# Batched matrix product on one core: x rounded to float16 before its transposes, two values to a float32 word

## The chip, the core and the metric

One core of a Trainium2 chip runs the whole program. Its TensorE (PE) multiplies and transposes, VectorE (DVE) and ScalarE (ACT) convert and copy, SyncE (SP) issues all transfers between the chip's memory (DRAM) and the core's own SBUF, and PSUM holds what TensorE writes. The metric is the device time of one execution in microseconds (us). Five executions of the kernel before took 135.75 to 136.54 us, median 136.04 us.

## What is computed

```python
def setup_inputs():
    batch, dim_i, dim_j, dim_k = 32, 256, 512, 384
    return {
        "x": np.random.randn(batch, dim_i, dim_j).astype(np.float32),
        "y": np.random.randn(batch, dim_j, dim_k).astype(np.float32),
    }

def reference(x, y):
    return np.einsum('bij,bjk->bik', x, y).astype(np.float32)
```

For each of 32 batches, a 256 x 512 matrix x times a 512 x 384 matrix y gives a 256 x 384 matrix. In float32 that is 16.8 MB of x, 25.2 MB of y and 12.6 MB of output, 54.5 MB in all.

## The kernel before

TensorE contracts over partitions, so both factors need j on the partitions. y comes from DRAM that way: partition p of a loaded y holds rows j = 4p to 4p+3, called t = 0 to 3 (NJ = 4). x arrives with rows i on the partitions and has to be transposed. Both are rounded to float16 on the way, the products add up in float32.

**Tiles.** x is loaded for four batches at a time (a quad q, 0 to 7): `x_sb`, 128 partitions by 8 rows (R = 8) by 512 columns, 2 MB in one transfer, line 66, three buffers. y is loaded for two batches (a step's pair u, 0 to 15), one transfer of 768 KB for each batch, line 81, five buffers `y_sb`. The output of a pair is one transfer of 768 KB, line 150, from `o_sb`.

**Transposes.** `transpose(q, half)`, lines 87 to 108, makes 16 transposes of 128 x 128 float32 for half of the four t (line 99): the columns j = 4c + t of one row r of `x_sb`, a stride of four elements. Four of them fill one PSUM tile `t_ps` (four buffers, 512 float32 per partition, one bank), and one copy takes the tile to `xt_sb` and rounds it to float16: DVE takes the even tiles (line 105), ACT the odd ones (line 107). A half has four tiles, so two copies on each engine.

**The rest of a step.** `round_y(u)` casts y to float16 in eight pieces of 384 columns, four on ACT (line 116) and four on DVE (line 118). `multiply(u)` makes 32 matmuls (line 130) into four PSUM tiles `o_ps` (four buffers): the two batches of the pair use the left and the right half of the array side by side, with 64 columns of `xt_sb` as weights each. `collect(u)` copies the four `o_ps` to `o_sb`, e = 0 and 2 on ACT (line 143), e = 1 and 3 on DVE (line 145). `store(u)` issues the output.

**Order.** Every instruction goes through `keep`, so each engine runs its own in the order of the source. Step s (0 to 17) does: load y of pair s+2 (with x of quad (s+3)/2 ahead of it when s is odd), collect(s-2), multiply(s-1), round_y(s), the first half of the next quad's transposes when s is odd and the second half when s is even and over 0, store(s-2). At s = 0 both halves of quad 0 come ahead of everything else. SP issues loads and stores in that one order: a store that waits for its copies holds back the loads behind it. There are eight semaphores for transfers, used in turn, so each issue also waits until the transfer eight places before it has landed.

**The end.** The last load issued is y of pair 15. Behind it stand five stores, of pairs 11 to 15. The last transposes are half 1 of quad 7, in step 14; after them come multiply(14), multiply(15), and their collects and stores.

Of the kernel before, what the change touches and what calls it, by code (L numbers as in the profile page):

```python
# [1 line left out]

# [5 lines left out]


MM_DT = mybir.dt.float16  # L10
F32 = mybir.dt.float32
P = 128


Q = 4
G = 2

LAG = 4


@with_exitstack
def kernel(
    ctx: ExitStack,
    tc: tile.TileContext,
    x: bass.AP,
    y: bass.AP,
    out: bass.AP,
):
    nc = tc.nc

    B, I, J = x.shape
    _, _, K = y.shape


    M = P // G
    NE = I // M
    NJ = J // P

    PQ = P // Q
    R = I // PQ
    H = R // NE
    U = B // G

    const_pool = ctx.enter_context(tc.tile_pool(name="const", bufs=1))
    x_pool = ctx.enter_context(tc.tile_pool(name="x_pool", bufs=3))
    y_pool = ctx.enter_context(tc.tile_pool(name="y_pool", bufs=5))
    yr_pool = ctx.enter_context(tc.tile_pool(name="yr_pool", bufs=2))
    xt_pool = ctx.enter_context(tc.tile_pool(name="xt_pool", bufs=2))  # L50
    o_pool = ctx.enter_context(tc.tile_pool(name="o_pool", bufs=5))
    tpsum_pool = ctx.enter_context(tc.tile_pool(name="tpsum", bufs=4, space=bass.MemoryType.PSUM))
    opsum_pool = ctx.enter_context(tc.tile_pool(name="opsum", bufs=4, space=bass.MemoryType.PSUM))


    keep = tc.keep_in_program_order

    identity = const_pool.tile([P, P], F32)
    make_identity(nc, identity)

    x_of, y_of, yr_of, xt_of, ps_of, o_of = {}, {}, {}, {}, {}, {}

    def load_x(q):
        x_of[q] = x_pool.tile([P, R, J], F32, name="x_sb")
        keep(
            nc.sync.dma_start(
                out=x_of[q],
                in_=x[q * Q : (q + 1) * Q].rearrange("g (p r) j -> (g p) r j", r=R),
            )
        )  # L70

    def load(u):

        if u == 0:
            load_x(0)
        if (u + 1) * G % Q == 0 and u + 1 < U:
            load_x((u + 1) * G // Q)
        y_of[u] = y_pool.tile([P, G, NJ, K], F32, name="y_sb")
        for g in range(G):
            keep(  # L80
                nc.sync.dma_start(
                    out=y_of[u][:, g],
                    in_=y[u * G + g].rearrange("(q t) k -> q t k", q=P),
                )
            )

    def transpose(q, half):

        x_sb = x_of[q]
        if half == 0:  # L90
            xt_of[q] = xt_pool.tile([P, NJ, NE, Q * PQ, H], MM_DT, name="xt_sb")
        n = 0
        for t in range(half * NJ // 2, (half + 1) * NJ // 2):
            for e in range(0, NE, 2):
                t_ps = tpsum_pool.tile([P, 2, H, Q * PQ], F32, name="t_ps")
                for f in range(2):
                    for h in range(H):
                        keep(
                            nc.tensor.transpose(  # L99
                                t_ps[:, f, h], x_sb[:, h * NE + e + f, t::NJ], identity  # L100
                            )
                        )
                dst = xt_of[q][:, t, e : e + 2].rearrange("c f p h -> c f h p")
                if n % 2 == 0:
                    keep(nc.vector.tensor_copy(dst, t_ps))  # L105
                else:
                    keep(nc.scalar.copy(dst, t_ps))  # L107
                n += 1

    def round_y(u):  # L110
        y_sb = y_of.pop(u)
        yr_of[u] = yr_pool.tile([P, G, NJ, K], MM_DT, name="y_r")
        for g in range(G):
            for t in range(NJ):
                if t % 2 == 0:
                    keep(nc.scalar.copy(yr_of[u][:, g, t], y_sb[:, g, t]))  # L116
                else:
                    keep(nc.vector.tensor_copy(yr_of[u][:, g, t], y_sb[:, g, t]))  # L118

    def multiply(u):  # L120
        xt_sb, y_r = xt_of[u * G // Q], yr_of.pop(u)
        ps_of[u] = []
        for e in range(NE):
            o_ps = opsum_pool.tile([P, K], F32, name="o_ps")
            ps_of[u].append(o_ps)
            for t in range(NJ):
                for g in range(G):
                    a = (u * G + g) % Q
                    keep(
                        nc.tensor.matmul(  # L130
                            o_ps[g * M : (g + 1) * M],
                            xt_sb[:, t, e, a * PQ : (a + 1) * PQ].rearrange("c p h -> c (p h)"),
                            y_r[:, g, t],
                            start=(t == 0),
                            stop=(t == NJ - 1),
                        )
                    )

    def collect(u):
        o_of[u] = o_pool.tile([P, NE, K], F32, name="o_sb")  # L140
        for e in range(NE):
            if e % 2 == 0:
                keep(nc.scalar.copy(o_of[u][:, e], ps_of[u][e]))  # L143
            else:
                keep(nc.vector.tensor_copy(o_of[u][:, e], ps_of[u][e]))  # L145
        del ps_of[u]

    def store(u):
        keep(
            nc.sync.dma_start(  # L150
                out=out[u * G : (u + 1) * G].rearrange("g (m e) k -> (g m) e k", e=NE),
                in_=o_of.pop(u),
            )
        )


    ahead = LAG - 2
    for u in range(ahead):
        load(u)
    for s in range(U + 2):  # L160
        if s + ahead < U:
            load(s + ahead)
        if s == 0:
            transpose(0, 0)
            transpose(0, 1)
        if s >= 2:
            collect(s - 2)
        if 1 <= s <= U:
            multiply(s - 1)
        if s < U:  # L170
            round_y(s)
        for half in range(2):
            q = (s + 1 - half) * G // Q
            if (s + 1 - half) * G % Q == 0 and 0 < q < B // Q:
                transpose(q, half)
        if s >= 2:
            store(s - 2)


# [1 line left out]
_INS = ['x', 'y']  # L181
_OUTS = [((32, 256, 384), 'float32')]


# [23 lines left out]
```

## Time and profile before

| what | value |
|---|---|
| median of 5 runs | 136.04 us |
| the profiled execution's own time | 135.99 us |
| its span in the trace | 134.1 us |
| granted TensorE clock, mean | 0.906 |
| bytes moved, mean rate over the span | 54.65 MB, 407 GB/s |
| L130 matmuls, 512 | 54.9 us busy |
| L99 transposes, 256 | 37.0 us busy |
| L118 / L116 casts of y, 128x384, 64 each | 20.0 us DVE, 355 ns each / 29.5 us ACT, 513 ns each |
| L105 / L107 copies of t_ps, 128x512, 32 each | 22.5 us DVE, 728 ns each / 22.4 us ACT, 731 ns each |
| L145 / L143 copies of o_ps, 128x384, 32 each | 16.3 us DVE, 543 ns each / 13.9 us ACT, 492 ns each |

The span runs from the first to the last event that the profiler recorded on the core; the execution's own time is 1.89 us longer. Busy time of an engine is the sum of its instructions' times, so two engines can both be busy at once. Times in the trace below are counted from the start of the span. A DMA share of 1 means that all 16 DMA engines that serve the core are moving data; rounding and overlap take it to 1.02 or so when none rests.

### The profile page before, as it was taken

Reading aid. Unit: us, or ns where it says so; the run is one execution under the profiler, and the core shown is the slowest. Engines: PE = TensorE matmul, PEld = TensorE weight load, DVE = VectorE, ACT = ScalarE, POOL = GpSimd, SP = SyncE. Lnnn points to the kernel's source line nnn. Section 1 sums busy time; section 2 is a strip of 40 time slices with the busy share of each in tenths; the row PEclk is TensorE's granted clock in tenths of the full one; section 3 lists DMA queues with packets and bytes.
Section 4 is the critical chain, followed back from the end, with each engine's and each line's share of the span. In section 5 each row is a group of like instructions: output and inputs, shape, how many; then the busy total and the mean of one; then the engine's idle time right before and its main releaser. Section 6 shows DMA issues by size and latency. Waiting matters only on the chain.

```text
span 134.1 us, 1968 instructions
## 1 busy us (share of the span) xinstructions
PE 91.0 (68%) x768; PEld 74.7 (56%) x768; DVE 56.2 (42%) x128; ACT 63.9 (48%) x129; POOL 0.7 (1%) x6
## 2 busy tenths in 40 slices
PE   0049494979199767786099771997739976597920
PEld 0049474868177666666077661676626766476810
DVE  0004617471743365701735318324273334628520
ACT  3004837662762476712744428424375245737710
POOL 2000000000000000000000000000000000000000
PEclk9999999999959999999968996589975799779997
DMA  5999999999999999999999999999999999999994
GB/s 112 410 407 453 401 423 421 440 405 416 410 459 393 419 425 420 449 399 418 423 437 439 400 421 429 441 425 404 427 418 456 399 417 425 418 432 416 425 396 169
DMA packets 8073, 54.65 MB, mean 407 GB/s; under 512 B 896, under 2 KB 896, under 8 KB 7040
## 3 DMA queue, kind: packets, MB, share of 16 engines
q1 hardware_dynamic: 8064, 54.53, 97.9%
q8 instruction: 6, 0.10, 0.3%
q14 instruction: 3, 0.02, 0.0%
HBM read 41.94 MB, written 12.58 MB: 407 GB/s over the span
## 4 chain that ended last, share of the span: by engine, by line
DMA 78%; PE 13%; ACT 4%; DVE 0%; issue 0%
DMA y_sb<-in_y_dram 40%; DMA x_sb<-in_x_dram 38%; PE o_ps L130 9%; PE t_ps L99 3%; ACT xt_sb L107 2%; ACT y_r L116 1%; ACT o_sb L143 1%; DVE o_sb L145 0%
## 5 line engine op out<-in xcount | busy, mean ns | idle before, releaser
L130 PE MATMUL o_ps<-y_r,xt_sb 128*64 128x384 f16 x512 | 54.9, 376 | 27.5 <-ACT o_sb L143 19.7
L130 PEld LDWEIGHTS <-xt_sb 128*64 128x64 f16 x512 | 40.4, 125 | 38.6 <-issue 21.4
L116 ACT CAST y_r<-y_sb 128x384 f16<-128x384 f32 x64 | 29.5, 513 | 36.5 <-DMA y_sb<-in_y_dram 36.3
L99 PE MATMUL t_ps<-identity,x_sb 128*128 128x128 f32 x256 | 37.0, 302 | 9.9 <-DMA x_sb<-in_x_dram 9.9
L99 PEld LDWEIGHTS t_ps<-identity,x_sb 128*128 128x128 f32 x256 | 34.3, 212 | 14.7 <-issue 14.7
L118 DVE CAST y_r<-y_sb 128x384 f16<-128x384 f32 x64 | 20.0, 355 | 44.4 <-DMA y_sb<-in_y_dram 44.4
L107 ACT CAST xt_sb<-t_ps 128x512 f16<-128x512 f32 x32 | 22.4, 731 | 25.9 <-PE t_ps L99 25.9
L105 DVE CAST xt_sb<-t_ps 128x512 f16<-128x512 f32 x32 | 22.5, 728 | 26.2 <-PE t_ps L99 26.2
L145 DVE COPY o_sb<-o_ps 128x384 f32<-128x384 f32 x32 | 16.3, 543 | 2.1 <-PE o_ps L130 2.1
L143 ACT COPY o_sb<-o_ps 128x384 f32<-128x384 f32 x32 | 13.9, 492 | 1.3 <-PE o_ps L130 1.3
L107 ACT ACT_TABLE_LOAD x1 | 1.3, 1283 | 0.7 <-PEq L192 0.7
masks.py:199 POOL TENSOR_SCALAR_AFFINE_SELECT identity<-identity 128x128 f32<-128x128 f32 x1 | 0.3, 294 | 0.1
masks.py:197 POOL MEMSET identity<- 128x128 f32 x1 | 0.2, 205 | 0.3 <-POOLq L192 0.3
L192 POOL MEMSET const-bfloat16-1.0<- 128x1 bf16 x1 | 0.1, 102 | 0.0
L192 POOL MEMSET const-uint8-127<- 128x1 uint8 x1 | 0.1, 102 | 0.0
L192 POOL MEMSET const-float32-0.0<- 128x1 f32 x1 | 0.1, 99 | 0.2 <-issue 0.2
L192 POOL MEMSET const-float32-1.0<- 128x1 f32 x1 | 0.1, 99 | 0.0
## 6 DMA issues: line engine op xcount, KB each, us to landing
y_sb<-in_y_dram SPq DMA_DIRECT2D x32, 768.0 KB, 17.9
x_sb<-in_x_dram SPq DMA_DIRECT2D x8, 2048.0 KB, 20.9
out_dram<-o_sb SPq DMA_DIRECT2D x16, 768.0 KB, 17.9
```

The costliest lines, as they stand in the source:

```text
L99: nc.tensor.transpose(t_ps[:, f, h], x_sb[:, h * NE + e + f, t::NJ], identity)
L105: keep(nc.vector.tensor_copy(dst, t_ps))
L107: keep(nc.scalar.copy(dst, t_ps))
L116: keep(nc.scalar.copy(yr_of[u][:, g, t], y_sb[:, g, t]))
L118: keep(nc.vector.tensor_copy(yr_of[u][:, g, t], y_sb[:, g, t]))
L130: nc.tensor.matmul(o_ps[g * M : (g + 1) * M], xt_sb[:, t, e, a * PQ : (a + 1) * PQ].rearrange("c p h -> c (p h)"), y_r[:, g, t], start=(t ...
L143: keep(nc.scalar.copy(o_of[u][:, e], ps_of[u][e]))
L145: keep(nc.vector.tensor_copy(o_of[u][:, e], ps_of[u][e]))
L192: nc = _bacc.Bacc("TRN2", target_bir_lowering=False, num_devices=1)
```

## The change

x of a quad is cast to float16 as soon as it is there, into a new tile `x_r` (two buffers): four casts of two rows, 128 x 1024 each, two on DVE and two on ACT. For quads 1 to 7 they stand in the odd steps ahead of round_y; for quad 0 they stand first. `x_r` is then read as float32 words, each of two neighbouring float16 values (j = 4c + 2n and 4c + 2n + 1), so a quad needs 16 transposes and not 32 (NW = 2 words in place of NJ = 4 columns). A half is now eight transposes in two `t_ps` tiles. Each tile holds 1024 float16 values per partition, and is copied out by two instructions of 512 values: f = 0 by DVE, f = 1 by ACT. `xt_sb` keeps the pairs side by side, so the weights of a matmul are read at a step of two elements where they were contiguous. Loads, stores, matmuls, casts of y and copies of the output are as they were. The core of the diff:

```diff
+    xr_pool = ctx.enter_context(tc.tile_pool(name="xr_pool", bufs=2))
...
+    def round_x(q):
+        xr_of[q] = xr_pool.tile([P, R, J], MM_DT, name="x_r")
+        for r in range(0, R, 2):
+            if r % 4 == 0:
+                keep(nc.vector.tensor_copy(xr_of[q][:, r : r + 2], x_of[q][:, r : r + 2]))
+            else:
+                keep(nc.scalar.copy(xr_of[q][:, r : r + 2], x_of[q][:, r : r + 2]))
+
     def transpose(q, half):
-        x_sb = x_of[q]
+        x_w = xr_of[q].bitcast(F32)
         if half == 0:
-            xt_of[q] = xt_pool.tile([P, NJ, NE, Q * PQ, H], MM_DT, name="xt_sb")
-        n = 0
-        for t in range(half * NJ // 2, (half + 1) * NJ // 2):
-            for e in range(0, NE, 2):
-                t_ps = tpsum_pool.tile([P, 2, H, Q * PQ], F32, name="t_ps")
-                for f in range(2):
-                    for h in range(H):
-                        keep(
-                            nc.tensor.transpose(
-                                t_ps[:, f, h], x_sb[:, h * NE + e + f, t::NJ], identity
-                            )
+            xt_of[q] = xt_pool.tile([P, NW, NE, Q * PQ, H, 2], MM_DT, name="xt_sb")
+        n = half
+        for e in range(0, NE, 2):
+            t_ps = tpsum_pool.tile([P, 2, H, Q * PQ], F32, name="t_ps")
+            for f in range(2):
+                for h in range(H):
+                    keep(
+                        nc.tensor.transpose(
+                            t_ps[:, f, h], x_w[:, h * NE + e + f, n::NW], identity
                         )
-                dst = xt_of[q][:, t, e : e + 2].rearrange("c f p h -> c f h p")
-                if n % 2 == 0:
-                    keep(nc.vector.tensor_copy(dst, t_ps))
+                    )
+            src = t_ps.bitcast(MM_DT).rearrange("c f h (p w) -> c f p h w", w=2)
+            dst = xt_of[q][:, n, e : e + 2]
+            for f in range(2):
+                if f == 0:
+                    keep(nc.vector.tensor_copy(dst[:, f], src[:, f]))
                 else:
-                    keep(nc.scalar.copy(dst, t_ps))
-                n += 1
+                    keep(nc.scalar.copy(dst[:, f], src[:, f]))
...
-                            xt_sb[:, t, e, a * PQ : (a + 1) * PQ].rearrange("c p h -> c (p h)"),
+                            xt_sb[:, t // 2, e, a * PQ : (a + 1) * PQ, :, t % 2].rearrange(
+                                "c p h -> c (p h)"
+                            ),
...
         if s == 0:
+            round_x(0)
             transpose(0, 0)
             transpose(0, 1)
         if s >= 2:
             collect(s - 2)
         if 1 <= s <= U:
             multiply(s - 1)
+        if (s + 1) * G % Q == 0 and s + 1 < U:
+            round_x((s + 1) * G // Q)
         if s < U:
             round_y(s)
```

In the built program the DVE and ACT instructions stand in the order of this source, and ACT's copy of a `t_ps` tile waits on a semaphore of DVE: its copy of f = 1 starts only after DVE's copy of f = 0 of the same tile is done. Before, the two engines copied different tiles and waited for TensorE alone.

## The prediction

> **What bounds the kernel now.** I read the page from its first part down, then the stretches of time, then the chain of waits, then SP's own rows.
>
> ```profile
> PE 91.0 (68%) x768; PEld 74.7 (56%) x768; DVE 56.2 (42%) x128; ACT 63.9 (48%) x129; POOL 0.7 (1%) x6
> ...
> DMA  5999999999999999999999999999999999999994
> ...
> q1 hardware_dynamic: 8064, 54.53, 97.9%
> ```
>
> No engine is busy for over 68% of the span, and the transfers take 97.9% of all 16 DMA engines' time. The row of digits says where the rest is: in the first slice and the last. The stretches show it closer (PE, PEld, DVE, ACT and POOL busy time, granted clock, DMA share, GB/s):
>
> ```profile
> 0.00:8.00 8.00, 0.00 (x0) 0.00 (x0) 0.00 (x0) 1.28 (x1) 0.70 (x6) 1.00 0.77 279
> ...
> 40.00:56.00 16.00, 13.18 (x124) 11.12 (x120) 8.01 (x18) 8.59 (x17) 0.00 (x0) 0.98 1.01 423
> ...
> 88.00:104.00 16.00, 12.19 (x100) 9.51 (x98) 7.03 (x16) 7.84 (x16) 0.00 (x0) 0.82 1.02 425
> ...
> 128.00:130.00 2.00, 0.36 (x6) 0.00 (x0) 0.56 (x1) 0.23 (x1) 0.00 (x0) 1.00 0.94 393
> 130.00:131.00 1.00, 0.00 (x0) 0.00 (x0) 0.00 (x0) 0.00 (x0) 0.00 (x0) 1.00 0.97 406
> 131.00:132.00 1.00, 0.00 (x0) 0.00 (x0) 0.00 (x0) 0.00 (x0) 0.00 (x0) 1.00 0.93 381
> 132.00:133.00 1.00, 0.00 (x0) 0.00 (x0) 0.00 (x0) 0.00 (x0) 0.00 (x0) 0.88 0.23 94
> ```
>
> With none resting the share is 1.02. The first 8 us lose 8 x (1 - 0.77/1.02) = 2.0 us before the first bytes: issued at 0.74, flowing 1.2 us later. Then nothing is lost until 128, whether TensorE's clock is 0.98 or 0.82: 423 and 425 GB/s. From 128 to 132 the loss is 2 x 0.08 + 0.05 + 0.09 = 0.3 of 1.02 us. So the time is a stream of bytes with a fixed start, and the compute engines matter only at its end, where the last bytes are made. There the chain of waits (start, us, what) reads:
>
> ```profile
> 112.98 0.93 ACT y_r L116 x2
> 113.90 1.21 ACT xt_sb L107 x2
> 115.11 0.35 ACT o_sb L143
> 115.46 0.04 issue
> 115.50 4.47 PE o_ps L130 x32
> 119.97 2.15 PE t_ps L99 x16
> 122.12 0.02 issue
> 122.15 0.73 ACT xt_sb L107
> 122.88 0.09 issue
> 122.97 5.41 PE o_ps L130 x64
> 128.38 0.02 issue
> 128.40 0.56 DVE o_sb L145
> ```
>
> The reader is to see a second chain that ends together with the bytes: y of pair 13 lands, its casts, the copies of transposes, a collect, multiply(13), the last 16 transposes, multiply(14) and (15), a copy. Then SP's rows:
>
> ```profile
> 23.81 0.35 SPq L150 DMA_DIRECT2D out_dram<-o_sb  x1
> ...
> 129.04 0.33 SPq L150 DMA_DIRECT2D out_dram<-o_sb  x1
> ```
>
> The last store is issued at 129.04. Were it alone, its 768 KB (0.786 MB) would flow from 130.2 (the 1.2 us of the start) for 1.9 us (at 423 GB/s), to 132.1. But work goes on to about 133, since some DMA engines still owe parts of the store before. So the last store could be some 1.0 us later before the end moves, and if it came earlier the slowest DMA engines, which never rested, would end where they do. This is the point that decides: the tail of compute has 1.0 us of room on one side, and on the other 0.3 us at most to win.
>
> **The change part by part.**
>
> *Transposes, 256 to 128.* 2.19 us for 16 at full clock (137 ns each), so 8 fewer in a half save 1.1 us of PE, 18 us in the whole. All halves but the last lie under the stream of bytes and are worth nothing. The last, of quad 7 in step 14, is on the tail's chain: -1.1 us there, if its copies follow as fast.
>
> *Copies of t_ps, still 64 of 512 values, now float16 in steps.* No such row is there. From below, packed values might go two at a time: half of 728 and 731, 0.36 us. From above, the 0.73 us of L105 and L107: the same count from the same memory, with the steps on the read and not on the write. I take 0.73, the nearest row. What is new is that ACT waits for DVE on each tile: DVE, then ACT, then (the second tile) ACT again, three copies in a row where two rows ran side by side. In the last half before, the first DVE copy began 0.78 us after the first transpose (119.91 to 120.69) and the last ACT copy ended at 122.88. After, from the same start: 120.69 + 3 x 0.73 = 122.88. So the saved 1.1 us is given back in full; at 0.36 the transposes end first and about 1.0 us is won. In step 13 the copies start together behind y's casts at 113.52: DVE to 114.2, ACT to 114.95, ACT to 115.65, then 0.35 for the collect: 116.0 where 115.46 stands, +0.5; at 0.36, 115.0, -0.5. Queued behind these ACT copies is the collect whose o_ps bank multiply(13) needs, so multiply(13) moves by that much. It ran 4.47 us, at half clock for most of it (32 matmuls take 2.79 us at full clock), so if the clock comes up when it did, half of the shift is absorbed: +0.25.
>
> *Casts of x, 16 each on DVE and ACT.* From below, the time of a 384-wide cast, 0.36 and 0.51 us; from above, in proportion to 1024, 0.95 and 1.37 us. I take the back-to-back rate of y's casts (0.63 and 0.93 us for two) in proportion: 0.84 and 1.24. DVE goes to 56 + 13 = 69 us, ACT to 64 + 20 = 84 of 134 us, both below the stream. They stand at the head of odd steps, waiting for x. Behind them wait y's casts, whose first half lands 2.0 us after x (109.27 and 111.23 for quad 7). ACT is then through at 109.27 + 2.5 = 111.75, half a microsecond late for the first half of y, and with that half done at 112.7 it is ready for the second, which lands at 112.95; at 1.37, 112.94, just in time. Price 0. The transposes wait for the casts, 111.75 in place of 110.75, but their copies cannot start before 113.5.
>
> *The start.* x lands at 8.49. With the casts, and 16 transposes at the slow clock that the 32 showed at first, the first matmuls begin within a microsecond of 15.87; then they may run at the slow clock, and the first store may come 2 us after its 23.81. What hides this are loads: the y of pair 3, issued before that store, lands in halves at 32.5 and 34.3, so the DMA engines have 10 us of work when SP waits there. In the later steps they have as much: a load takes 17.9 us from issue to landing. x's buffers come free earlier (casts, not transposes, end their use), and the queue of SP is the same.
>
> *Weights at a step of two.* L99 loads 128 columns at a step of 16 bytes in 125 ns (2.00 us for 16), L130 loads 64 contiguous ones in 76 ns (2.44 us for 32). A step does not show in these, so 0; from above, twice 2.44 us for 32 would exceed the 2.79 us of a multiply and add 2.1 to each of the last two, 4.2 in the tail.
>
> *The clock.* In the first transposes the tiles of four come 0.85 us apart up to 13.2 us and 0.48 apart after, with no matmul yet: transposes alone brought the clock up, in under 5 us. So half as many leave TensorE more idle, above all in odd steps, where its rest before a multiply grows from 2.55 us (to 115.50) to about 3.5. The slow stretch at 115.5 may thus be longer.
>
> [...]
>
> **Sum.** In the tail +0.25 (step 13) and 0 (step 14): last store at 129.3, inside its 1.0 us of room, so the end moves by 0. Span 134.1, with 1.89 around it 135.99, and the median of the runs lies 0.05 above: 136.04, rounded 136.0. With the low price of copies the tail is 1.3 us earlier, and the end gains 0.3 at most: 135.7. Runs before reach from -0.3 to +0.5 of their median, so 135.6 to 136.7 is the likely case's own range. A change within 0.3% (0.4 us) is about what can't be told from none here.
>
> **Rivals.**
>
> *The tail runs at the slow clock (slower).* The rest before multiply(13), longer by a microsecond, lets the slow stretch last through it and into multiply(14). For it: the stretch of 116 to 120 had a clock of 0.61 already, and in 99.48 to 104.81 all 32 matmuls ran slow, 5.33 us in place of 2.79. Against: PE then works from 116 to 121 nearly without rest, and did come up in that time before. Price: one multiply slow to its end, 2.5 us, less the 1.0 of room: +1.5, 137.5. It decides once the last store is issued later than 130.0. Chance 0.15.
>
> *The end follows the tail (faster).* If bytes were not what ends the span, the 1.1 us of transposes would come off: 134.9. For it: the chain above has them in it. Against: the share of 0.93 to 0.97 up to 132. Chance 0.13.
>
> *The casts become the bound.* ACT at 84 us, were the work in step 13 to wait for it: the store of pair 11 would be late, but five stores' room lies behind it. Nothing in the odd steps comes near 16 us per quad: 84/8 is 10.5. Its time would be 136.4 at most (+0.4, y's second half cast later by that). Chance 0.02, and it counts as no change.
>
> **How the numbers follow.** No change, by the bytes: 0.70, and that gives the time, 136.0. With the rivals: faster 0.13 and 0.01 from the low end of the likely case, slower 0.15 and 0.01 from weights; same 0.70. The range is that of the likely case, down to 135.5 for a part of the faster one and up to 136.9 for a mild form of the slow clock, one third of its price beyond the room.
>
> **What would show it.** Right: the rate stays at 407 GB/s over the span, the DMA share at 1.01 or 1.02 from 16 to 128; 128 transposes, about 18 us; x casts near 0.84 and 1.24 us; ACT's copies behind DVE's; the last store issued between 128.0 and 130.0; the chain still made of transfers. Wrong: a stretch before 128 with a DMA share under 1, a last store after 130, or copies of t_ps far from 0.73 us together with an end that moved by more than 0.4.

## The result and the profile after

The changed kernel takes 136.49 us (median of 30 runs, 136.20 to 136.87); the kernel before, run beside it, 136.13 us (57 runs, 135.75 to 136.95). The ratio is 1.0025, with a 95% interval of 1.0018 to 1.0032: slower by a little. That is less than the 0.3% that I had taken as no change, but with so many runs it is told apart from none. The profiled execution of the changed kernel took 136.39 us, its span 134.6 us.

The first parts of the changed kernel's page (busy time, the slices of the DMA engines, the queues):

```profile
PE 82.1 (61%) x640; PEld 59.1 (44%) x640; DVE 57.4 (43%) x144; ACT 75.8 (56%) x145; POOL 0.7 (1%) x6
...
DMA  5999999999999999999999999999999999999991
...
q1 hardware_dynamic: 8064, 54.53, 97.5%
q8 instruction: 5, 0.08, 0.2%
q14 instruction: 2, 0.02, 0.0%
```

PE gave up 8.9 us, ACT took on 11.9. None of it is near the span, and the data queue q1 is as full as before. The stretches of time (columns as before: PE, PEld, DVE, ACT, POOL, granted clock, DMA share, GB/s):

```profile
0.00:8.00 8.00, 0.00 (x0) 0.00 (x0) 0.00 (x0) 1.28 (x1) 0.70 (x6) 1.00 0.77 281
...
40.00:56.00 16.00, 11.74 (x89) 7.97 (x86) 7.18 (x18) 9.31 (x18) 0.00 (x0) 0.80 1.01 420
88.00:104.00 16.00, 10.52 (x80) 7.23 (x79) 7.18 (x18) 9.31 (x18) 0.00 (x0) 0.79 1.02 426
...
128.00:130.00 2.00, 0.09 (x2) 0.00 (x0) 0.56 (x1) 0.00 (x0) 0.00 (x0) 1.00 0.93 390
130.00:131.00 1.00, 0.00 (x0) 0.00 (x0) 0.00 (x0) 0.00 (x0) 0.00 (x0) 1.00 1.01 418
```

The stream of bytes is the one of before: the same 0.77 at the start, 1.01 to 1.02 from 16 to 104 us and 0.98 from 104 to 112 in both, at a lower clock of TensorE (mean 0.875 for 0.906). The tail of compute, on TensorE in order of time (start, us, what, idle time before):

```profile
114.95 4.23 PE L145 MATMUL o_ps<-y_r,xt_sb 128*64 128x384 f16 x32 [2.94 <-DVE o_sb L162]
119.11 1.22 PE L113 MATMUL t_ps<-identity,x_r 128*128 128x128 f32 x8
121.41 2.79 PE L145 MATMUL o_ps<-y_r,xt_sb 128*64 128x384 f16 x32 [1.07 <-DVE o_sb L162]
125.30 2.79 PE L145 MATMUL o_ps<-y_r,xt_sb 128*64 128x384 f16 x32 [1.10 <-DVE o_sb L162]
```

and the last store in SP's rows:

```profile
128.75 0.33 SPq L167 DMA_DIRECT2D out_dram<-o_sb  x1
```

multiply(13) begins at 114.95, where 115.50 stood before; the last store is issued at 128.75, 0.29 us earlier than the 129.04 of before. So the tail did not hold up the end. The chain of waits agrees: from 12.20 to 124.12 it is made of transfers but for 0.2 us, and its end (start, us, what) reads

```profile
109.33 14.80 DMA y_sb<-in_y_dram
...
124.78 0.48 DVE o_sb L162
125.25 0.04 issue
125.30 2.81 PE o_ps L145 x32
```

multiply(14) began 1.56 us earlier than before (121.41 for 122.97). But the last y landed at 124.12, DVE's casts of it stand ahead of the copy that multiply(15) waited for, and so only 0.29 us of this reached the last store.

Yet the span is 0.5 us longer. Where is it? What is left is the stretch behind the last landing, where SP has waited for the last store and the engines meet to close the program. The rows of the instructions that wait for the end and close it (durations min/median/max in ns, first to last start in us), first of the kernel before, then of the changed one:

```profile
L203 SPq EVENT_SEMAPHORE  x7: 17/28/28, 129.8 to 134.1; - x7
...
L203 SPq DRAIN  x3: 7/7/7, 133.4 to 133.7; - x3
```

```profile
L223 SPq EVENT_SEMAPHORE  x7: 17/28/28, 129.1 to 134.6; - x7
...
L223 SPq DRAIN  x3: 7/7/130, 133.7 to 134.2; - x3
```

One DRAIN of SP took 130 ns where all three took 7, and the first of them stands at 133.7 where it stood at 133.4. SP's records one by one show it plainly (number from 0, start us, ns, us since the end of the one before):

```
before   78  129.04   332  0.04  DMA_DIRECT2D     (the last store)
         79  129.80    28  0.43  EVENT_SEMAPHORE
         83  133.30    28  1.78  EVENT_SEMAPHORE  (the last store has landed)
         84  133.37     7  0.04  DRAIN
after    73  128.75   332  0.03  DMA_DIRECT2D     (the last store)
         74  129.14    28  0.06  EVENT_SEMAPHORE
         78  133.30    28  1.79  EVENT_SEMAPHORE  (the last store has landed)
         79  133.73   130  0.40  DRAIN
         83  134.55    17  0.38  EVENT_SEMAPHORE  (the end)
```

The last landing ended SP's wait at 133.30 in both. In both, SP stood still for 0.4 us ahead of its record no. 79. Before, no. 79 was the first wait behind the last store. The two transfers that it waits for had landed by 125.98, so its 0.43 us is no wait for them; and with the last store's bytes still on their way, the stall cost nothing. After, no. 79 is the DRAIN behind the last wait, and everything waits for it: 0.40 - 0.04 of stall and 0.12 more of the DRAIN itself, 0.48 us. That is the whole difference of the spans (134.1 and 134.6).

Why has SP five records fewer? The rows of the x loads, before and after:

```profile
L66 SPq DMA_DIRECT2D x_sb<-in_x_dram x8: 327/328/672, 0.7 to 88.4; - x8
L66 SPq EVENT_SEMAPHORE  x5: 17/17/17, 24.2 to 88.3; - x5
```

```profile
L70 SPq DMA_DIRECT2D x_sb<-in_x_dram x8: 328/328/573, 0.7 to 88.4; - x8
```

Before, a load of x into a buffer in use waited both for the transfer eight places before it and for PE's transposes, and the second wait was an instruction of its own, five times. Now the readers of x_sb are casts on DVE and ACT, and that second wait is gone from the program: SP has 84 records in the trace where it had 89 (86 and 91 in the expectations below, which count two more that the trace does not hold). Why it is gone is argued, not shown: by then SP has waited, for a store, for later copies on the same two engines, so a wait for the casts would be idle.

The theory, then: SP stalls for some 0.4 us at a fixed place in its stream of instructions, the change moved this place behind the last landing, and the work that the change adds and removes costs nothing. The rival: the work costs it (casts, copies, a lower clock), and the stall at the end is chance.

### The profile page after: what moved, and what is told of

It reads as the page before. It is cut to its first block, busy times and chain, and to the rows that moved or that the text cites. A ratio compares the mean times of both kernels' runs of the same rounds, so it can differ in the third digit from the quotient of the medians.

```text
span 134.6 us, 1741 instructions
## 1 busy us (share of the span) xinstructions
PE 82.1 (61%) x640; PEld 59.1 (44%) x640; DVE 57.4 (43%) x144; ACT 75.8 (56%) x145; POOL 0.7 (1%) x6
## 3 DMA queue, kind: packets, MB, share of 16 engines
q1 hardware_dynamic: 8064, 54.53, 97.5%
## 4 chain that ended last, share of the span: by engine, by line
DMA 91%; PE 2%; DVE 1%; SPq 1%; issue 0%; DVEq 0%
DMA y_sb<-in_y_dram 62%; DMA x_sb<-in_x_dram 16%; DMA out_dram<-o_sb 13%; PE o_ps L145 2%; DVE o_sb L162 1%; SPq L85 0%; DVE y_r L133 0%; SPq L70 0%; SPq L167 0%; DVEq L162 0%
## 5 line engine op out<-in xcount | busy, mean ns | idle before, releaser
L145 PE MATMUL o_ps<-y_r,xt_sb 128*64 128x384 f16 x512 | 58.5, 393 | 31.3 <-DVE o_sb L162 29.4
L113 PE MATMUL t_ps<-identity,x_r 128*128 128x128 f32 x128 | 24.2, 324 | 14.7 <-DVE x_r L95 14.6
L113 PEld LDWEIGHTS t_ps<-identity,x_r 128*128 128x128 f32 x128 | 18.9, 210 | 22.1 <-issue 12.3
L97 ACT CAST x_r<-x_sb 128x1024 f16<-128x1024 f32 x16 | 15.9, 1043 | 19.0 <-DMA x_sb<-in_x_dram 19.0
L123 ACT COPY xt_sb<-t_ps 128x512 f16<-128x512 f16 x32 | 17.4, 588 | 13.4 <-DVE xt_sb L121 12.9
L95 DVE CAST x_r<-x_sb 128x1024 f16<-128x1024 f32 x16 | 10.4, 690 | 25.1 <-DMA x_sb<-in_x_dram 25.1
L121 DVE COPY xt_sb<-t_ps 128x512 f16<-128x512 f16 x32 | 12.9, 420 | 12.9 <-PE t_ps L113 12.5
```

What stands on the lines that cost most here:

```text
L95: keep(nc.vector.tensor_copy(xr_of[q][:, r : r + 2], x_of[q][:, r : r + 2]))
L97: keep(nc.scalar.copy(xr_of[q][:, r : r + 2], x_of[q][:, r : r + 2]))
L113: nc.tensor.transpose(t_ps[:, f, h], x_w[:, h * NE + e + f, n::NW], identity)
L121: keep(nc.vector.tensor_copy(dst[:, f], src[:, f]))
L123: keep(nc.scalar.copy(dst[:, f], src[:, f]))
L145: nc.tensor.matmul(o_ps[g * M : (g + 1) * M], xt_sb[:, t // 2, e, a * PQ : (a + 1) * PQ, :, t % 2].rearrange("c p h -> c (p h)"), y_r[:, g ...
```

## The experiments

Each was timed against the kernel before on the same chip. "Around the span" is the execution's time less its span, averaged over a kernel's runs: 1.81 us for the changed kernel's runs and 1.80 to 1.82 for those of before.

**Five more instructions on SP, then one.** A drain on SP is one more instruction that moves no data; the five of e1, each right behind the issue of a store, took 124 to 134 ns, long before the end.

```diff
 # after                                  e1: s in (4, 5, 6, 7, 8)    e2: s in (4,)
         if s >= 2:
             store(s - 2)
+        if s in (4,):
+            keep(nc.sync.drain())
```

> The changed kernel with five empty instructions (drains) more on SP, one at the end of each of steps 4 to 8, so that SP has 91 instructions as before the change and not 86. Boundary theory (SP stalls 0.4 us ahead of the 79th recorded instruction of its stream; the change has taken five instructions out ahead of it, so that the stall fell behind the landing of the last store): the stall goes back ahead of the landing, the span is 134.1 and the time 136.1, as before the change. Work theory (casts of x, copies and clock cost the 0.36 us): no change, 136.5.

> The changed kernel with a single drain more on SP, in step 4. Boundary theory: the stall moves by one instruction, from the drain behind the last wait to the last wait itself, which lasts 1.8 us anyway, so one instruction is enough: 136.1, and the gap of 0.4 us stands ahead of SP's last wait for a store. Work theory: 136.5.

Measured: e1 136.04 us (ratio 0.9991, 0.9979 to 1.0003), e2 136.03 us (0.9989, 0.9975 to 1.0003). One instruction more on SP takes the whole loss back. In e1's trace no. 79 is again the first wait behind the last store, 0.42 us after the issue. In e2's trace the row of the closing DRAINs reads

```profile
L225 SPq DRAIN  x3: 7/7/7, 133.5 to 133.8; - x3
```

and SP's record no. 79 is now the wait for the last store itself, in which a stall does not show. Nothing that computes differs between e2 and the changed kernel, so the casts, copies and the clock can't be what made that 136.49.

**The same done to the kernel before.** If the place is a matter of SP's count, the kernel before must lose by it too: 123 drains more should put a place 128 instructions further on where it hurts; 5 should put no. 79 elsewhere, at no cost. The 128 is an estimate that the traces of both kernels give. Of the two queues that the page calls instruction, q8 moves packets of 16384 bytes, six before and five after. If they belong to TensorE's 1536 and 1280 matmuls, transposes and weight loads, they are 64 bytes for each; the packets of q14 have 8192 bytes, 128 times that.

```diff
 # before                                 e4: one each in steps 4 to 8
         if s >= 2:
             store(s - 2)
+        if s in (3, 4, 5, 6, 7, 8, 9, 10, 11):
+            for _ in range(15 if s < 11 else 3):
+                keep(nc.sync.drain())
```

> The kernel before with 123 drains more on SP, 15 in each of steps 3 to 10 and 3 in step 11, nothing else changed. The instruction packets of the profile's smaller queue are 8192 bytes, that is 128 instructions of 64 bytes if they are that long; then boundaries are 128 apart, and 123 = 128 - 5 puts the next one where the changed kernel has its own. Boundary theory with a distance of 128: 136.5, with the gap of 0.4 us at the same instruction as in the changed kernel. With another distance, or by the work theory: 136.1, since 15 drains of some 0.05 us (0.75 us a step) lie in SP's waits of over 6 us a step.

> A control: the kernel before with five drains more on SP in steps 4 to 8. Boundary theory: the stall moves five instructions earlier, to the issue of a store that is waiting anyway: 136.1. Work theory: 136.1 too. If drains themselves cost time, over 136.1.

Measured: e3 136.64 us (1.0035, 1.0016 to 1.0053), e4 136.24 us (1.0002, 0.9981 to 1.0023). The row of e3:

```profile
L206 SPq DRAIN  x3: 7/7/131, 134.5 to 134.9; - x3
```

The long DRAIN is there again, 131 ns, with 0.34 us of stall ahead of it, and it is SP's record no. 207 = 79 + 128. In e4, SP's no. 79 is the issue of the store of pair 13, 0.42 us after the wait before it ended (0.30 in the kernel before, so most of it is no stall). The first wait behind the last store, which had the 0.43 us ahead of it before, now has 0.05, and nothing is lost. So the place belongs to SP's count and not to the work, and the next one is 128 instructions on. One thing in e3 is not as clean as it sounds: its profiled execution, 137.12 us, also issued the last store late, at 130.7. Its median of 136.64 may hold some of that besides the stall; of its other executions only the time, the span and the clock are known.

**The room of the tail.** The prediction gave the last store 1.0 us of room. The kernel before, with its last copy of the output made once more (e6) or four times more (e7):

```diff
                     keep(nc.vector.tensor_copy(o_of[u][:, e], ps_of[u][e]))
+                if u == U - 1 and e == NE - 1:
+                    for _ in range(4):
+                        keep(nc.vector.tensor_copy(o_of[u][:, e], ps_of[u][e]))
```

> The kernel before, with the last copy of the last output (DVE, 0.5 us) done a second time, so that the last store is issued at 129.55 and not 129.04. The room predicted is 1.0 us: 136.1, no change. If the tail had no room: +0.5, 136.6.

> The kernel before, with the last copy of the last output done four times more, so that the last store is issued 2.0 us later, at about 131.0. With a room of 1.0 us: +1.0, 137.1. If the end followed the tail from the start: +2.0, 138.1. If the DMA engines' backlog is larger than thought: under +0.5.

Measured: e6 136.39 us (1.0026, 1.0003 to 1.0049), in two groups, six runs at 135.88 to 136.15 and six at 136.63 to 137.42; e7 137.62 us (1.012, 1.0095 to 1.0144). SP's rows of e7, the last store and the closing DRAINs:

```profile
131.30 0.33 SPq L153 DMA_DIRECT2D out_dram<-o_sb  x1
```

```profile
L206 SPq DRAIN  x3: 7/7/7, 135.0 to 135.3; - x3
```

The store is issued 2.26 us later than in before (129.04), the DRAIN comes 1.6 us later (133.4): the room is about 0.6 us, not 1.0. Two other traces give 0.7 (e6: store 1.39 later, its DRAIN 0.73) and 0.9 (e3: store 1.71 later, its landing 0.79). For e6 the outcome depends on more than its one copy: in its profiled execution (136.63 us) the last store came at 130.43, 1.39 later for 0.56 us of copy, with the clock at 0.50 from 116 to 120. For the changed kernel neither matters; its last store is early.

**Fewer instructions on SP by another way.** In the changed kernel, y of pairs 4, 6, 8, 10 and 12 loaded by one transfer each where there were two: SP's place should move on by five, behind the end.

```diff
+        if u in MERGED:                        # MERGED = (4, 6, 8, 10, 12)
+            keep(nc.sync.dma_start(out=y_of[u], in_=y[u * G : (u + 1) * G].rearrange("g (q t) k -> q g t k", q=P)))
+            return
```

> The changed kernel with five fewer instructions on SP: y of pairs 4, 6, 8, 10 and 12 comes in one transfer of 1536 KB and not in two of 768. SP has 81 instructions, so the place of the stall, the 79th recorded one, lies behind the last one that the profile records. Boundary theory: the gap ahead of the drain is gone from the span, 134.1; if the launch's own code behind the span pays it instead, the time stays 136.5, if not it is 136.1. Work theory: 136.5, with a span of 134.6.

Measured: 136.60 us (1.0021, 1.0003 to 1.0038), in two groups, five runs at 136.06 to 136.24 and seven at 136.57 to 136.95. A miss as a test. The DRAINs of its profiled execution (136.95 us) are as the theory has them, 7 ns each,

```profile
L233 SPq DRAIN  x3: 7/7/7, 134.4 to 134.7; - x3
```

but the last store was issued at 129.53 and the last wait took 4.2 us (128.75 and 1.8 in the changed kernel): larger transfers changed the tail as well as the count, and the time says nothing on either theory. The time around the span stayed at 1.80 us, so SP's place did not show there either.

**What the casts cost.** With the stall out of the way (the one drain of e2), the added work can be priced by doubling it: every cast of x twice (e5), DVE's alone (e9), ACT's alone (e10), and e2's kernel again beside them as their zero (e11).

```diff
 # e9; e10 has the loop around the cast on ACT, e5 around both
             if r % 4 == 0:
-                keep(nc.vector.tensor_copy(xr_of[q][:, r : r + 2], x_of[q][:, r : r + 2]))
+                for _ in range(2):
+                    keep(nc.vector.tensor_copy(xr_of[q][:, r : r + 2], x_of[q][:, r : r + 2]))
```

> The changed kernel with one drain more on SP (as in the second experiment, which ran 136.03 us), and every cast of x done twice into the same place: 26 us more on DVE and ACT together. Boundary theory, with the bytes as the bound: nothing of it is seen but what reaches the tail. ACT's four casts of quad 7 end at 109.3 + 4.0 = 113.3, so y's casts and multiply(13) start 1.3 us later, and the last store goes from 128.74 to at most 130.0, just inside the room of 1.0 us after 129.04: 136.0 to 136.1. Work theory: the casts' cost is paid a second time, 136.4 or more.

> The changed kernel with one drain more on SP, as in e2, and only DVE's 16 casts of x made twice (+16 x 0.69 = 11 us of DVE). If the +0.3 us of e5 is the price of the work itself, spread over both engines, DVE's part is some 11 of 27.7 us: 136.15 us. If it is one engine's instruction stream or one engine's late casts, this kernel shows all of it (136.35) or nothing (136.04).

> The same with only ACT's 16 casts of x made twice (+16 x 1.04 = 17 us of ACT). If the price is spread as the work is, 136.22 us. If it is one engine's, this kernel shows all of it (136.35) where e9 shows nothing, or nothing (136.04) where e9 shows all.

> The kernel of e2 beside e9 and e10 on their chip, as their zero: 136.04 us by every theory. If it comes out at 136.3 or above here, e5's +0.3 was the chip and the day and not the casts, and the boundary's 0.45 us would be in doubt too.

| kernel | median us | ratio to before, 95% | median span | around the span |
|---|---|---|---|---|
| e11, one drain | 136.08 | 1.0002 (0.9987 to 1.0018) | 134.3 | 1.81 |
| e10, ACT's casts twice | 136.26 | 1.0009 (0.9993 to 1.0024) | 134.4 | 1.82 |
| e5, all casts twice | 136.37 | 1.0020 (1.0010 to 1.0030) | 134.3 | 2.03 |
| e9, DVE's casts twice | 136.54 | 1.0027 (1.0014 to 1.0039) | 134.5 | 2.05 |

e11 repeats e2. e5 was a surprise to my theory, which gave 136.0 to 136.1. Most of it comes with DVE's doubled casts: e9 lies 0.46 us above e11, e10 only 0.18, which the intervals don't tell from nothing nor from the price of ACT's share. The last two columns say where: 0.2 us of e5 and e9 is not in the span at all. No cast runs there. Common to the two is that DVE has 16 instructions more, so I asked whether DVE has such places too. In the changed kernel DVE stands still for 0.46 us ahead of its record no. 63, a cast of y whose transfer had landed 0.53 us before (0.46 to 0.48 us at no. 63 in e1, e2, e8 and e11 too). 128 further on is no. 191; DVE's records in e9 end with no. 181, so that place, if there is one, would fall behind the span. To test it, e12 gives DVE still more to do:

```diff
                     keep(nc.vector.tensor_copy(xr_of[q][:, r : r + 2], x_of[q][:, r : r + 2]))
+                for _ in range(4 if 1 <= q <= 6 else 0):
+                    keep(nc.vector.tensor_copy(xr_of[q][:, r, :16], x_of[q][:, r, :16]))
```

> The kernel of e9 with still more work on DVE: in quads 1 to 6, each cast of two rows is followed by four casts of 16 values that write the same values again, 48 short instructions in all. In e5 and e9 the span stayed at 134.3 to 134.5 us, and the time around it rose from 1.81 to 2.03 and 2.05 us (every other kernel: 1.78 to 1.82). If DVE's instruction stream has boundaries 128 apart like SP's (one shows as 0.46 us at DVE's instruction 63 in the changed kernel's trace), the next lies at 191; e9's DVE ends at 181 in the span, so the boundary would fall into the code behind it. With 48 more it lies some 40 instructions before the end, under the stream of bytes: 1.81 us around the span again, 136.1 to 136.3 us, so faster than e9 for more work. If the doubled work itself costs the 0.4 us, or the number of DVE's instructions: 136.5 us or more, with 2.04 or more around the span.

Measured: 136.28 us (1.0014, 0.9996 to 1.0033), median span 134.5, and 1.78 us around it: every run between 1.73 and 1.86, where those of e9 lay between 1.99 and 2.13. More work, and the 0.2 us is gone. The small instruction queue in the profiles of e9 and of e12 (packets, MB, share):

```profile
q14 instruction: 3, 0.02, 0.1%
```

```profile
q14 instruction: 4, 0.03, 0.1%
```

e12 has one packet more, of 8192 bytes at 104.89 us, when DVE stands between its no. 188 (which ends at 103.08) and no. 189 (105.08): a packet near the place that was looked for, and now inside the span; DVE waits for TensorE there, so a stall could not show. So of the 0.29 us that e5 lost to e11, and of the 0.46 of e9, some 0.22 lies outside the span and goes away when DVE's count is moved, as a place in DVE's stream would have it. Where it lies is not shown: the semaphore events that the traces hold behind the span come at the same times in e5 as in e2, the last one 1.90 us after its end, and SP's place behind the span in e8 cost nothing there. What is left, 0.1 to 0.2 us in the spans of e9, e10 and e12, lies inside the scatter of these runs; whether twice the casts cost that much stays open. That the change as a whole, its casts included, costs nothing once the stall is out of the way is what e1, e2 and e11 show: the changed kernel then takes the time of the kernel before.

## Why the prediction was wrong, by its own steps

**The step that failed** is in *The start*: "x's buffers come free earlier (casts, not transposes, end their use), and the queue of SP is the same." The first half is right and goes with what makes the second wrong. With x_sb read by casts on DVE and ACT, five waits for TensorE are gone, each an instruction of SP, and with them SP's place of stall moved by five, from under the last store's bytes to behind their landing. The sum then kept "1.89 around it" and what follows the last landing as fixed: "the end moves by 0". By the landing it did move by 0 (SP's last wait ends at 133.30 in both). The code behind the landing grew by 0.48 us. The prediction read SP's rows only for stores and for how long each waited; it did not count SP's instructions, and no rival was about them. Its time, 136.0, is what e1, e2 and e11 took (136.03 to 136.08); that 136.49 lies inside its range owes nothing to its reasons, since the range reached up to 136.9 for a slow clock. Nor do its bounds follow from its own terms: -0.3 and +0.5 around 136.0 give 135.7 and 136.5, not 135.6 and 136.7, and a third of the 1.5 us beyond the room is 0.5, which gives 136.5, not 136.9.

**Bytes bound it, and the transposes are hidden: right.** DMA share 1.01 to 1.02 from 16 us to 104, 97.5% for q1. PE lost 8.9 us of busy time and the last landing came no sooner. That "nothing is lost until 128" was a little too much: in both kernels the share was 0.98 from 104 to 112, some 0.3 us.

**Copies of t_ps: too dear.** I took 0.73 us, the upper bound. The two groups of copies in the changed kernel's page, and those of the casts:

```profile
L97 ACT CAST x_r<-x_sb 128x1024 f16<-128x1024 f32 x16 | 15.9, 1043 | 19.0 <-DMA x_sb<-in_x_dram 19.0
L123 ACT COPY xt_sb<-t_ps 128x512 f16<-128x512 f16 x32 | 17.4, 588 | 13.4 <-DVE xt_sb L121 12.9
L95 DVE CAST x_r<-x_sb 128x1024 f16<-128x1024 f32 x16 | 10.4, 690 | 25.1 <-DMA x_sb<-in_x_dram 25.1
L121 DVE COPY xt_sb<-t_ps 128x512 f16<-128x512 f16 x32 | 12.9, 420 | 12.9 <-PE t_ps L113 12.5
```

(mean ns of one behind the busy time). DVE's copy takes 420 ns, nearer to the low bound of 0.36; ACT's 588, between. That low bound was my estimate, half of 728 and 731 ns; no run shows values going two at a time. The serial order that I expected is there: ACT's copies wait 12.9 us for DVE's. In step 13 that order eats up what the prices save: ACT's collect starts at 115.00, as before (114.97). But multiply(13) no longer waits for that collect. What released it, at 114.81, was DVE's first one, where before it was ACT's at 115.46; so it begins 0.55 us earlier than before and not 0.5 later. That the bank would be one that ACT frees was taken over from the trace before; why it is another one now is not shown.

**Casts of x: dear too, and free as said.** 690 and 1043 ns for the 0.84 and 1.24 taken. In step 13, ACT's two end at 111.32 (111.75 forecast) and DVE's at 110.62; y's first half was cast from 111.3 on and its second, landing at 113.0, set the rest, as the prediction had it. The rival by which the casts become the bound is out with that: ACT was busy for 75.8 us, not 84.

**The tail: inside its room, but with the wrong sign.** +0.25 forecast, -0.29 measured. Its room was 0.6 to 0.9 us (e7, e6, e3) where I said 1.0; none of it was used.

**The start: hidden, as said.** The first 16 transposes took 3.99 us (9.27 to 13.26), all at the slow pace (tiles of four 0.85 us apart; the granted clock in the rows reads 1.00 from 8 to 16 us in both kernels and does not show it), and the first store came at 23.7 as before (23.8).

**Weights at a step of two: right.** The loads took 132 ns each where they took 125, 6% more with the mean clock 3% lower. At full clock 32 of them take 2.45 us where they took 2.44, and a multiply still takes 2.79 us.

**The clock: fell, as I had thought it could, and did not matter.** Mean granted clock 0.875 for 0.906, and 0.845 to 0.876 in all runs of the changed kernel, against 0.89 to 0.95 in the runs of the kernel before that stand beside the experiments. The matmuls' busy time rose from 54.9 to 58.5 us. Fewer transposes and a lower clock go together here, but the work around them changed too, so what lowered it is not shown. The first rival, a tail at the slow clock, asked for a last store after 130.0; it was at 128.75. The rest before multiply(13) did grow, 2.55 to 2.94 us, and multiply(13) was slow for most of its length, 4.23 us, as before (4.47).

**The end follows the tail: no.** The tail came 0.29 us earlier and the last landing stayed.

## What to carry to other kernels

Where bytes bound a kernel and its end is a wait for the last transfer, the few instructions behind that wait are on the critical path (133.30 to 134.06 us before, to 134.55 after): look at them in both traces before looking for a cause in the work. A difference of half a microsecond there (0.48 us in this case) may come from how many instructions an engine has had before, so add or take away one instruction that does nothing and see whether the difference goes. And compare the span and the time around it each by itself: e5 and e9 lost 0.2 us where no row of the trace could show it.

## What the runs showed of the hardware

SP stands still for 0.34 to 0.43 us ahead of its recorded instructions no. 79 (0.43 before, 0.40 after, 0.42 in e1) and, in e3, no. 207 (0.34), 128 further on; in e2 and e4, where the place lies in a wait or right behind one, it does not show. A closing DRAIN behind the stall took 130 ns where the others took 7; that alone is no sign, since drains right behind the issue of a store took 123 to 134 ns with no stall. DVE stands still for 0.46 us ahead of its no. 63 in the changed kernel, and what e9 and e12 show fits a second place near no. 191. The trace holds small packets of 8192 bytes on the queue q14 that follow these places: for SP at 132.19 us in the kernel before, at 134.62 in the changed one (behind its end, which is why its page counts two where the kernel before has three), at 126.61 in e4, each time 0.9 to 3 us after the stall, and in e3 at 135.11, 0.6 us after it. 8192 bytes for 128 instructions are 64 bytes each, as many as the packets of q8 give by the estimate ahead of e3 (16384 bytes for 256 of TensorE's). The traces show the place, one distance of 128 on SP, the stall and the packet; what SP and DVE wait for there is not shown. Where nothing covered it, the stall cost 0.48 us, in the changed kernel.
